# Making two of seven half-size products ahead for every pair of feature tiles, in place of the plain up-projection of a gated MLP, in an fp32 decoder trunk

## The chip, the cores and the metric

The kernel runs on one core of one Trainium2 chip. The metric is the device time of one launch in microseconds (us): the median of several runs of the same build. A profile is one execution recorded by the hardware profiler. Of the engines, PE is TensorE (matmuls; PEld is its weight load), DVE is VectorE, ACT is ScalarE, SP is SyncE, whose queue issues nearly all DMAs of this kernel.

## The reference

Two layers over 1024 tokens of width 1024, all in fp32. Layer 0 mixes tokens by gated recurrence and attention, layer 1 by pooling; each layer then has a gated MLP, and its up- and down-projection are what the change is about:

```python
h = x * (1.0 + sc2) + sh2                # x: after the mixer and a layer norm
u, v = jnp.split(h @ w_up, 2, axis=-1)   # w_up: 1024 x 5632, u and v: 1024 tokens x 2816
uc = conv_b                              # causal depthwise conv of width 3 along the tokens
for j in range(CONV_WIDTH):
    uc = uc + up[:, j:j + T] * conv_w[j]     # up: u with two zero rows ahead
y = (jax.nn.silu(uc) * v) @ w_down       # w_down: 2816 x 1024
x = _layer_norm(ALPHA * x + g2 * y, ln_g[l, 1], ln_b[l, 1])
```

The vectors `sc2`, `sh2`, `g2` and their like (adaLN) come from the conditioning vector `c` by a matrix of 1024 x 6144 per layer.

## The kernel before

Features lie on the 128 partitions and tokens along the row. The 1024 tokens are two halves of 512 (`hf` 0 and 1), the width 1024 is 8 tiles of 128 (`KT`), the 2816 features are 22 tiles (`FT`); tile `i` of u and of v make one gated feature tile. Every fp32 operand is split in a high part, a cast made by ACT (L261), and a low part, a subtraction made by DVE (L262). A product of two operands is three matmul passes (high by high, high by low, low by high), so a projection of 512 tokens to 128 features is 8 x 3 = 24 matmuls of 128x128 by 128x512.

**The plain up-projection.** `up` (L912) makes one feature tile for one half of the tokens: 24 matmuls into `pu`, the conv (`conv`, L896: ACT scales, DVE adds the two shifted terms, ACT applies silu), 24 matmuls into `pv`, a product with v on DVE, and a store of the result in DRAM (`hidden`). `STD = (5, 9)` of the 22 tiles go this way in layer 0 and in layer 1: 4 x 24 = 96 matmuls for one tile.

**The pairs.** The other 17 and 13 tiles go through `paired` (L971). It takes u and v of a tile and both halves of the tokens as a 2 by 2 block product, and makes it with seven half-size products instead of eight (Strassen's scheme, Winograd's form). Each is a `product` (L958) of 12 matmuls, and a tile is 84. The left factors are a11, a12, a22 (blocks of w_up) and s1 to s4 (sums of them, made by `pair_weights`, L218, on DVE); the right ones are b11, b21, b22 (blocks of h) and t1 to t4 (`forms`, L928: loaded again from DRAM, added on DVE, split). a11 b11 + a12 b21 is u of the first half. The results are put together by DVE: u2 and v2 are u and v of the second half, v1 is v of the first.

**Down.** `down` (L1012) loads `hidden` again (`load_hidden`, tiles `gh`, `gl`, `gt`), splits it, and multiplies with granules of w_down that are loaded and split once for each half of the tokens.

**Order.** The program is one long Python trace; the framework's scheduler keeps its own order on each engine. `weight` and `fetch` (L239, L253) load and split weights in the order of use, two ahead. Beside the main loop (L1173 to L1192) run generators: `tick` (L97) advances them at a rate given to `start`, and so lays their instructions between the matmuls. `norm_prep` and `between` (L1148, L1129) hold layer norm, pooling and `ffn_prep` (L871), which makes h of one half, splits it and stores it; for the second half they run beside the plain up-projection of the first, and `forms` beside that of the second. `fill` (L165) lays the making of adaLN vectors between the matmuls: one `ada_tile` is a DMA of 512 KB and a DVE reduce (L142), 96 in all. Tiles of 512 columns come from a pool `t2` of 25 buffers, staged weights from `ws` of 4, split weights from `wh` of 4, PSUM from two pools of 4 banks.

Of the kernel before, what the change touches and what calls it, by code (L numbers as in the profile page):

```python
# [17 lines left out]
P = 128  # L18
# [24 lines left out]
T2_BUFS = 25  # L43
# [9 lines left out]
STD = (5, 9)  # L53
FILL = 0.5
# [4 lines left out]
def trunk(ctx: ExitStack, tc: tile.TileContext, a: dict, out: bass.AP):  # L59
# [12 lines left out]
    def t2(name, w=HT):  # L72
        return tp.tile([P, HT + 16], F32, tag="t2", name=name, bufs=T2_BUFS)[:, :w]

# [22 lines left out]
    def tick():  # L97
        for item in list(active):
            item[2] += item[1]
            while item[2] >= 1:  # L100
                item[2] -= 1
                if next(item[0], active) is active:
                    active.remove(item)
                    break
# [75 lines left out]

    def parts(st, n=1024, hl=None):
# [4 lines left out]
        split(hl[0][:, :n], hl[1][:, :n], st[:, :n])  # L186
        return hl

# [10 lines left out]
    for l in range(DEPTH):  # L199
        for hf in range(NH):  # L200
            for i in range(STD[l]):
                worder += [("w_up", l, i), ("w_up", l, FT + i)]
        worder += [("pair", l, i) for i in range(STD[l], FT)]
# [7 lines left out]
    fetched = []  # L211

# [5 lines left out]
    def pair_weights(l, i):  # L218
# [3 lines left out]
        ga = parts(wa)  # L222
# [126 lines left out]
    def modulate(n, j, sv, tv, hl, act=False, keep=None):  # L349
# [7 lines left out]
        if keep is not None:  # L357
            nc.sync.dma_start(keep, hf)
# [495 lines left out]
    def outproj(hf):  # L854
        o = o_hl[hf]
        need((0, 2))
        rs_[hf] = r = [t2(f"r{hf}_{j}") for j in range(KT)]
# [13 lines left out]
    def ffn_prep(l, hf):  # L871
# [5 lines left out]
        h = hs[hf] = hl8(f"hf{l}{hf}")  # L877
        for j in range(KT):
            hsp[l, hf, j] = dram(f"h{l}{hf}{j}")
            rsp[l, hf, j] = dram(f"r{l}{hf}{j}")  # L880
            modulate(n[j], j, sv, tv, h, keep=hsp[l, hf, j])
            S.activation(n[j], n[j], AF.Identity, bias=col(bv, j), scale=col(av, j))
            nc.sync.dma_start(rsp[l, hf, j], n[j])
            yield
# [11 lines left out]
    def conv(l, i, u, first, last):  # L896

        uc = t2("uc")
# [13 lines left out]
    def up(l, hf, i):  # L912

        h = hs[hf]
        act = lambda k, hi: h[k][:, hi, :]
        pu = mm("pu")
        gemm(pu, weight("w_up", l, i), act, KT)
        tick()
        uc = conv(l, i, pu, uh[:, i, :] if hf else None, None if hf else uh[:, i, :])
        pv = mm("pv")  # L920
        gemm(pv, weight("w_up", l, FT + i), act, KT)
        V.tensor_tensor(uc, uc, pv, ALU.mult)
        nc.sync.dma_start(hidden(l, hf, i), uc)
        tick()

    right = {}

    def forms(l):  # L928

        for nm in ("t1", "t2", "t4", "t3"):  # L930
            right[nm] = []
        for k in range(HK):
            b11, b21, b12, b22 = (t2("hb") for _ in range(4))
            for t, (hf, kk_) in ((b11, (0, k)), (b12, (1, k)), (b22, (1, HK + k)), (b21, (0, HK + k))):
                nc.sync.dma_start(t, hsp[l, hf, kk_])
# [34 lines left out]

    def paired(l):  # L971
# [3 lines left out]
        low = [[(hs[hf][k][:, 0, :], hs[hf][k][:, 1, :]) for k in range(KT)] for hf in range(NH)]  # L975
        b11, b21, b22 = low[0][:HK], low[0][HK:], low[1][HK:]
        prev = None

        def ends(q):
            i, w, s1, y, z, u1, u2, v2, uc1 = q  # L980
            product(y, w["a22"], right["t4"], False, True)
            v1 = t2("v1")
            V.tensor_tensor(v1, s1, y, ALU.add)
            V.tensor_tensor(uc1, uc1, v1, ALU.mult)
            nc.sync.dma_start(hidden(l, 0, i), uc1)
            product(z, w["s4"], b22, False, True)
            V.tensor_tensor(u2, u2, z, ALU.add)
            uc2 = conv(l, i, u2, u1[:, HT - 2 : HT], None)
            V.tensor_tensor(uc2, uc2, v2, ALU.mult)
            nc.sync.dma_start(hidden(l, 1, i), uc2)  # L990

        for i in range(STD[l], FT):
            w = weight("pair", l, i, ahead=1)
            x, y, z = mm("px"), mm("py"), ax("pz")
            s1, u1, u2, v2 = (t2(nm) for nm in ("s1", "u1", "u2", "v2"))
            product(x, w["a11"], b11, True, True)
            S.copy(s1, x)
            product(y, w["s2"], right["t2"], True, True)
            V.tensor_tensor(u2, s1, y, ALU.add)
# [3 lines left out]
            product(x, w["a12"], b21, False, True)  # L1003
            S.copy(u1, x)
# [3 lines left out]
            uc1 = conv(l, i, u1, None, None)  # L1008
            prev = i, w, s1, y, z, u1, u2, v2, uc1
        ends(prev)  # L1010

    def down(l, hf):  # L1012
# [3 lines left out]
        g = []  # L1016

        def load_hidden():
# [7 lines left out]
        n = rs_[hf] = [t2(f"r{l}{hf}_{j}") for j in range(KT)]  # L1026
        for j0 in range(0, KT, 2):
# [237 lines left out]
```

## Time and profile before

| | |
|---|---|
| median of 3 runs | 1966.31 us (1966.2 to 1967.88) |
| the profiled execution, its own time | 1964.34 us |
| its span | 1962.5 us |
| mean granted clock of TensorE | 0.989 |
| PE busy | 1902.8 us (97%), 9558 matmuls |
| DVE busy | 1469.6 us (75%) |
| ACT busy | 821.5 us (42%) |
| DMA | 286.72 MB, 146 GB/s on average |

An engine's busy time is the time in which it carried out at least one instruction; instructions of one engine overlap a little, so the sum of their durations is larger. The chain of work that ended last goes back from the last instruction to what released each step, and gives each engine its share of the span. The 1.8 us between span and own time lie around the program.

### The profile page before, as it was taken

Reading aid. Unit: us, or ns where it says so; the run is one execution under the profiler, and the core shown is the slowest. Engines: PE = TensorE matmul, PEld = TensorE weight load, DVE = VectorE, ACT = ScalarE, POOL = GpSimd, SP = SyncE. Lnnn points to the kernel's source line nnn. Section 1 sums busy time; section 2 is a strip of 40 time slices with the busy share of each in tenths; the row PEclk is TensorE's granted clock in tenths of the full one; section 3 lists DMA queues with packets and bytes.
Section 4 is the critical chain, followed back from the end, with each engine's and each line's share of the span. In section 5 each row is a group of like instructions: output and inputs, shape, how many; then the busy total and the mean of one; then the engine's idle time right before and its main releaser. Section 6 shows DMA issues by size and latency. Waiting matters only on the chain.

```text
span 1962.5 us, 25481 instructions
## 1 busy us (share of the span) xinstructions
PE 1902.8 (97%) x9558; PEld 1590.4 (81%) x9558; DVE 1469.6 (75%) x2737; ACT 821.5 (42%) x1240; POOL 0.2 (0%) x4
## 2 busy tenths in 40 slices
PE   6999999999999999999999899998999999999996
PEld 6988988888788888888787678877888888888786
DVE  6897678778888787887755898998667777732846
ACT  4654254434664333343412435545434343422522
POOL 0000000000000000000000000000000000000000
PEclk9999999999999999999999899998999999999998
DMA  9522232234564333334775555336422222643731
GB/s 311 196 102 76 98 108 86 82 124 161 204 247 139 115 122 122 119 119 134 263 256 187 190 173 205 112 109 228 161 76 91 81 81 80 223 153 101 254 112 44
DMA packets 101932, 286.72 MB, mean 146 GB/s; under 512 B 12976, under 2 KB 15408, under 8 KB 101808
## 3 DMA queue, kind: packets, MB, share of 16 engines
q1 hardware_dynamic: 101232, 284.56, 42.4%
q8 instruction: 75, 1.23, 0.2%
q10 hardware_dynamic: 576, 0.52, 0.1%
q14 instruction: 49, 0.40, 0.1%
HBM read 241.00 MB, written 44.04 MB: 145 GB/s over the span
## 4 chain that ended last, share of the span: by engine, by line
PE 87%; DVE 6%; DMA 4%; ACT 2%; issue 1%; SPq 0%; DVEq 0%; ACTq 0%
PE pd L1039 20%; PE py L961 12%; PE pz L961 8%; PE px L961 8%; PE pu L271 8%; PE pv L271 7%; PE op L271 4%; PE zt L497 4%; PE att L740 3%; PE zt L395 2%; PE pd L271 2%; DMA wst<-g 2%; PE aq L271 1%; DVE whl L262 1%; PE pp L1123 1%
## 5 line engine op out<-in xcount | busy, mean ns | idle before, releaser
L261 ACT CAST whl<-wst 128x1024 fp32r<-128x1024 f32 (+1 forms) x267 | 271.5, 1029 | 477.8 <-PE pd L1039 180.1
L262 DVE TENSOR_TENSOR whl<-wst,whl 128x1024 fp32r<-128x1024 f32 (+1 forms) x267 | 316.0, 1194 | 92.9 <-ACT whl L261 91.6
L1039 PE MATMUL pd<-gh,whl 128*128 128x512 f32 x1024 | 322.1, 393 | 1.6 <-ACT gh L261 1.0
L961 PE MATMUL py<-t,whl 128*128 128x512 f32 x1080 | 258.1, 392 | 0.0
L961 PEld LDWEIGHTS py<-t,whl 128*128 128x128 f32 x1080 | 202.6, 188 | 45.2 <-DVE v L1006 0.6
L1039 PEld LDWEIGHTS pd<-gh,whl 128*128 128x128 f32 x1024 | 193.3, 189 | 43.9 <-ACT gh L261 1.7
L1039 PE MATMUL pd<-gl,whl 128*128 128x512 f32 x512 | 201.5, 393 | 8.4 <-DVE gl L262 8.4
L271 PE MATMUL pu<-hf,whl 128*128 128x512 f32 x672 | 166.0, 400 | 9.2 <-ACT uh L908 6.2
L961 PE MATMUL px<-hf,whl 128*128 128x512 f32 x720 | 173.8, 390 | 0.0
L271 PEld LDWEIGHTS pu<-hf,whl 128*128 128x128 f32 x672 | 129.5, 193 | 37.6 <-ACT uh L908 6.6
L961 PEld LDWEIGHTS px<-hf,whl 128*128 128x128 f32 x720 | 135.2, 188 | 29.1
L271 PE MATMUL pv<-hf,whl 128*128 128x512 f32 x672 | 158.5, 390 | 0.0
L142 DVE CUSTOM_DVE_ANT_0 adast<-adast,c 128x1024 f32<-128x1024 f32 x96 | 117.2, 1223 | 54.6 <-DMA adast<-in_ada_wT 54.4
L271 PEld LDWEIGHTS pv<-hf,whl 128*128 128x128 f32 x672 | 126.0, 188 | 26.3
L1039 PEld LDWEIGHTS pd<-gl,whl 128*128 128x128 f32 x512 | 96.9, 189 | 30.3 <-DVE gl L262 10.0
L1039 PE MATMUL pd<-gt,whl 128*128 128x512 f32 x432 | 102.6, 392 | 1.0 <-ACT gt L261 1.0
L497 PE MATMUL zt<-whl,h 128*128 128x256 f32 x768 | 100.7, 286 | 0.0
L902 DVE SCALAR_TENSOR_TENSOR uc<-u,cw,uc 128x511 f32<-128x511 f32 x120 | 89.8, 748 | 12.4 <-ACT uc L899 11.6
L1039 PEld LDWEIGHTS pd<-gt,whl 128*128 128x128 f32 x432 | 81.0, 188 | 19.2 <-ACT gt L261 1.4
L497 PEld LDWEIGHTS zt<-whl,h 128*128 128x128 f32 x768 | 94.4, 191 | 0.7 <-issue 0.3
L271 PE MATMUL op<-o,whl 128*128 128x512 f32 x384 | 91.8, 394 | 0.0
L961 PE MATMUL pz<-hf,gs 128*128 128x512 f32 x360 | 88.9, 395 | 0.0
(243 smaller groups left out, 2758.1 us busy)
## 6 DMA issues: line engine op xcount, KB each, us to landing
wst<-in_w_up SPq DMA_DIRECT2D x116, 512.0 KB, 3.5
adast<-in_ada_wT SPq DMA_DIRECT2D x96, 512.0 KB, 4.1
wst<-in_w_dn SPq DMA_DIRECT2D x64, 512.0 KB, 4.4
g<-uc SPq DMA_DIRECT2D x88, 256.0 KB, 2.0
wst<-g SPq DMA_DIRECT2D x44, 512.0 KB, 4.3
r<-r SPq DMA_DIRECT2D x64, 256.0 KB, 3.9
wst<-in_w_tok SPq DMA_DIRECT2D x28, 512.0 KB, 4.2
wst<-in_w_dn SPq DMA_DIRECT2D x32, 384.0 KB, 3.7
```

What stands on the lines that cost most here:

```text
L142: V.tensor_tensor_reduce(out=w, in0=w, in1=cb, scale=1.0, scalar=0.0, op0=ALU.mult, op1=ALU.add, accum_out=col(mods[l, ch], k),)
L261: S.copy(hi, src)
L262: V.tensor_tensor(lo, src, hi.bitcast(F32), ALU.subtract)
L271: PE.matmul(ps, w[wi][:, k * P : (k + 1) * P], act(k, hi), start=i == 0, stop=i == n - 1)
L395: PE.matmul(ps[t // 2][:, (t % 2) * 256 : (t % 2 + 1) * 256], h[k][:, hi, t * P : (t + 1) * P], w[wi][:, (k % 4) * 256 : (k % 4 + 1) * 256 ...
L497: PE.matmul(ps[:, u * 256 : (u + 1) * 256], h[k_][:, hi, (t + u) * P : (t + u + 1) * P], w[k_ // 4][wi][:, (k_ % 4) * 256 : (k_ % 4 + 1) * ...
L740: PE.matmul(ps[:, s], lhs[:, s], rhs[:, s], start=True, stop=True)
L902: V.scalar_tensor_tensor(uc[:, sh:], u[:, : HT - sh], cw, uc[:, sh:], ALU.mult, ALU.add)
L961: PE.matmul(ps, w[wi][:, k * P : (k + 1) * P], blk[k][hi], start=start and k == pi == 0, stop=stop and k == HK - 1 and pi == 2, skip_group ...
L1039: PE.matmul(ps[jj], w[jj][wi][:, (k - c0) * P : (k - c0 + 1) * P], act(k, hi), start=k == pi == 0, stop=k == sum(last_k) - 1 and pi == 2,)
L1123: PE.matmul(ps, wg[wi][:, b : b + P], o[k][:, hi, :], start=i == 0, stop=i == 5)
```

## The change

`STD` and `up` are gone: all 22 tiles of a layer go through the seven products. `EARLY = (16, 22)` tiles of each layer are cut in two. `early(l)` makes for each of them the two products a11 b11 and a12 b21, 24 matmuls, which need the first half of the tokens alone. It copies the first product (`s1`, ACT) and, after the second, u of the first half (`u1`, or for tiles from `EARLY_CONV = (0, 12)` on its conv result `uc`) and stores both in DRAM, by ACT's DMA queue. `paired(l)` loads them again and makes the other five products of these tiles, 60 matmuls ("late"), and all seven of the rest, six in layer 0.

In `paired`, ACT now copies s1 into the PSUM bank `y` ahead of s2 t2, and the matmuls add to it; DVE's additions of s1 (L983, L999, L1006) fall away, and ACT copies u2 and v2 out of PSUM. v2 + y, made by DVE, now has to be read before a22 t4 is added to the same bank.

Beside `early(l)` now run `norm_prep(1)` or `between(1)` and `forms` after it (`rest`), at the rates 1.5 and 2.5, and `issue_after` lays their instructions behind the split of the next weight. Smaller parts: `ffn_prep` of the second half doesn't split the four blocks that no product uses, and makes every other h of the first half on ACT; `pool_mix` makes `he` on ACT; `down` stores the low halves of w_down's granules in DRAM at the first half and loads them at the second (`again`), where before DVE made them a second time; `load_hidden` of the second half runs in the last quarter of the first; adaLN is filled at a rate of 0.65 (before 0.5) up to the MLP and 0.4 (before 0.2) in `paired`; `t2` has 19 buffers, a new pool `e2` 6.

```diff
+PIN = 1
+EARLY = (16, 22)
+EARLY_CONV = (0, 12)
-STD = (5, 9)
...
+    def again(src, key, n, hl):
...
+        nc.sync.dma_start(hl[1][:, :n].bitcast(F32), wlo[key])
+        st = wp.tile([P, 1024], F32, tag="ws", name="wst", bufs=WS_BUFS)
+        nc.sync.dma_start(st[:, :n], src)
+        S.copy(hl[0][:, :n], st[:, :n])
         return hl
...
+    def early(l):
+        b11, b21 = half_blocks(0)
+        prev = None
+        def end(q):
+            i, w, x = q
+            product(x, w[1], b21, False, True)
+            if i < EARLY_CONV[l]:
+                uc = e2("u1")
+                S.copy(uc, x)
+                S.copy(uh[:, i, :], uc[:, HT - 2 : HT])
+            else:
+                uc = conv(l, i, x, None, uh[:, i, :], e2("uc"))
+            kept[l, i, 1] = dram(f"e{l}{i}")
+            nc.scalar.dma_start(kept[l, i, 1], uc)
+        for i in range(EARLY[l]):
+            g = weight("w_up", l, i, ahead=min(3, EARLY[l] - i))
+            w = [tuple(z[:, q * 512 : (q + 1) * 512] for z in g) for q in range(2)]
+            behind[:] = splits.get(("w_up", l, i + PIN), [])
+            x, s1 = mm("px"), e2("s1")
+            product(x, w[0], b11, True, True)
+            S.copy(s1, x)
+            kept[l, i, 0] = dram(f"s{l}{i}")
+            nc.scalar.dma_start(kept[l, i, 0], s1)
+            if prev is not None:
+                end(prev)
+            prev = i, w, x
...
-        def ends(q):
-            i, w, s1, y, z, u1, u2, v2, uc1 = q
+        def end1(q):
+            i, w, y, z, u1, uc1, u2, v2 = q
             product(y, w["a22"], right["t4"], False, True)
-            v1 = t2("v1")
-            V.tensor_tensor(v1, s1, y, ALU.add)
-            V.tensor_tensor(uc1, uc1, v1, ALU.mult)
+            V.tensor_tensor(uc1, uc1, y, ALU.mult)
             nc.sync.dma_start(hidden(l, 0, i), uc1)
+        def end2(q):
+            i, w, y, z, u1, uc1, u2, v2 = q
             product(z, w["s4"], b22, False, True)
             V.tensor_tensor(u2, u2, z, ALU.add)
...
+        for i in range(FT):
+            late = i < EARLY[l]
+            w = weight("late" if late else "pair", l, i, ahead=1)
+            x, y, z = None if late else mm("px"), mm("py"), ax("pz")
+            u2, v2 = t2("u2"), t2("v2")
+            if late:
+                s1, u1 = nxt
+                nxt = load_kept(i + 1)
+                S.copy(y, s1)
+            else:
+                u1 = t2("u1")
+                product(x, w["a11"], b11, True, True)
+                S.copy(y, x)
+                if prev is not None:
+                    end1(prev)
+            product(y, w["s2"], right["t2"], False, True)
+            S.copy(u2, y)
             if prev is not None:
-                ends(prev)
+                (end1 if late else end2)(prev)
             product(z, w["s1"], right["t1"], True, True)
+            S.copy(v2, z)
+            if late:
+                if prev is not None:
+                    end2(prev)
+            else:
+                product(x, w["a12"], b21, False, True)
+                S.copy(u1, x)
             product(y, w["s3"], right["t3"], False, True)
-            V.tensor_tensor(v2, s1, y, ALU.add)
-            V.tensor_tensor(v2, v2, z, ALU.add)
+            V.tensor_tensor(v2, v2, y, ALU.add)
...
+                    if hf == 0 and j0 == KT - 2 and k % 2:
+                        load_hidden(nxt, 1)
...
     for l in range(DEPTH):
-        for hf in range(NH):
-            if hf:
-                finish(pb_)
-                pb_ = start(forms(l), 0.7)
-            for i in range(STD[l]):
-                up(l, hf, i)
+        early(l)
         finish(pb_)
-        pace[0] = 0.2
+        pace[0] = 0.4
         paired(l)
```

The order of instructions moves at two places. The first is DVE in the middle of `paired(0)`: what it does between one addition of a product in `pz` and the next addition of one in `py`. `whl` and `gs` are low halves of weights, `wsum` the sums of weight blocks, `cw0` the conv weights. Before:

```order
L987 TENSOR_TENSOR u2_6366<-u2_6366,pz_6363 128x512
L150 TENSOR_TENSOR mod05_92<-mod05_92,ada_bT_81 128x8
L902 SCALAR_TENSOR_TENSOR uc_6568<-u2_6366,cw0_641,uc_6568 128x511
L904 SCALAR_TENSOR_TENSOR uc_6568<-u1_6365,cw0_641,uc_6568 128x1
L902 SCALAR_TENSOR_TENSOR uc_6568<-u2_6366,cw0_641,uc_6568 128x510
L262 TENSOR_TENSOR whl_6494<-wsum_6488,whl_6494 128x1024
L904 SCALAR_TENSOR_TENSOR uc_6568<-u1_6365,cw0_641,uc_6568 128x2
L224 TENSOR_TENSOR wsum_6632<-wst_6627 128x512
L225 TENSOR_TENSOR wsum_6632<-wsum_6632,wst_6625 128x512
L262 TENSOR_TENSOR whl_6497<-wst_6483,whl_6497 128x1024
L989 TENSOR_TENSOR uc_6568<-uc_6568,v2_6367 128x512
L1006 TENSOR_TENSOR v2_6509<-s1_6506,py_6504 128x512
```

The same piece after the change, in a late tile:

```order
L1076 TENSOR_TENSOR u2_6624<-u2_6624,pz_6623 128x512
L297 TENSOR_TENSOR gs_6730<-s4_6721,gs_6730 128x512
L251 TENSOR_TENSOR wsum_6828<-wst_6826 128x512
L946 SCALAR_TENSOR_TENSOR uc_6798<-u2_6624,cw0_641,uc_6798 128x511
L948 SCALAR_TENSOR_TENSOR uc_6798<-uh_701,cw0_641,uc_6798 128x1
L946 SCALAR_TENSOR_TENSOR uc_6798<-u2_6624,cw0_641,uc_6798 128x510
L948 SCALAR_TENSOR_TENSOR uc_6798<-uh_701,cw0_641,uc_6798 128x2
L1109 TENSOR_TENSOR v2_6736<-v2_6736,py_6733 128x512
L252 TENSOR_TENSOR wsum_6828<-wsum_6828,wst_6824 128x512
L1078 TENSOR_TENSOR uc_6798<-uc_6798,v2_6625 128x512
```

Six instructions now stand between the addition to u2 and the one to v2, where ten stood; the conv of u2 is still ahead of the latter.

The second is ACT at the passage from `down(0, 0)` to `down(0, 1)`. Granules of 768 columns are the last of a pair of output tiles, `gh` is hidden of the second half. Before:

```order
L261 CAST whl_9197<-wst_9195 128x768
L261 CAST whl_9202<-wst_9200 128x768
L261 CAST whl_9261<-wst_9259 128x1024
L261 CAST whl_9266<-wst_9264 128x1024
L261 CAST gh_9334<-wst_9332 128x1024
L261 CAST gh_9340<-wst_9338 128x1024
L261 CAST whl_9324<-wst_9322 128x1024
L261 CAST whl_9329<-wst_9327 128x1024
L261 CAST gh_9346<-wst_9344 128x1024
```

And after the change:

```order
L297 CAST gh_9344<-wst_9342 128x1024
L297 CAST gh_9362<-wst_9360 128x1024
L297 CAST gh_9380<-wst_9378 128x1024
L297 CAST gh_9398<-wst_9396 128x1024
L297 CAST whl_9404<-wst_9402 128x768
L297 CAST whl_9411<-wst_9409 128x768
L297 CAST gh_9430<-wst_9428 128x1024
L297 CAST gh_9448<-wst_9446 128x1024
L297 CAST gh_9466<-wst_9464 128x1024
L297 CAST gh_9484<-wst_9482 128x1024
L199 CAST whl_9488<-wst_9490 128x1024
```

Eight casts of hidden now stand ahead of the second half's first granule (`whl_9488`, made by `again`), which itself came ahead of all of them before.

## Rows read from the trace of the kernel before

**Rows 1.** The page: busy times and shares of the chain that ended last.

```profile
PE 1902.8 (97%) x9558; PEld 1590.4 (81%) x9558; DVE 1469.6 (75%) x2737; ACT 821.5 (42%) x1240; POOL 0.2 (0%) x4
PE 87%; DVE 6%; DMA 4%; ACT 2%; issue 1%; SPq 0%; DVEq 0%; ACTq 0%
```

**Rows 2.** Chain of waits, plain up-projection of both layers: start, us, what.

```profile
507.13 7.33 PE pu L271 x24
...
581.57 5.44 PE pv L271 x24
...
1220.99 5.49 PE pu L271 x24
...
1345.41 8.29 PE pu L271 x24
```

**Rows 3.** Chain of waits, one pair of layer 0, and the end of layer 1's.

```profile
641.64 5.60 PE pz L961 x24
647.24 2.76 PE px L961 x12
...
660.99 5.60 PE pz L961 x24
...
1697.82 110.42 PE pd L1039 x485
```

**Rows 4.** Timeline of PE, end of layer 0's pairs: start, us, engine, line, operation, tiles.

```profile
949.38 0.40 PE L1039 MATMUL pd<-gl,whl 128*128 128x512 f32 x1
```

**Rows 5.** Windows: stretch, length, busy (instructions) of PE, PEld, DVE, ACT, POOL; clock; DMA share, GB/s.

```profile
619.60:953.00 333.40, 333.40 (x1449) 271.68 (x1448) 269.30 (x409) 134.15 (x175) 0.00 (x0) 1.00 0.37 125
1221.00:1345.00 124.00, 115.39 (x508) 93.53 (x507) 117.02 (x202) 64.21 (x93) 0.00 (x0) 0.98 0.38 133
```

**Rows 6.** Timeline of DVE: layer norm, pooling and plain up-projection of layer 1.

```profile
1249.46 4.87 DVE L333 TENSOR_TENSOR r<-r,rstd 128x512 f32<-128x512 f32 x8 [0.86 <-PE rstd L330]
1254.25 0.54 DVE L1093 TENSOR_SCALAR he<-r,v,v 128x512 f32<-128x512 f32 x1
1254.70 1.23 DVE L262 TENSOR_TENSOR whl<-wst,whl 128x1024 fp32r<-128x1024 f32 x1
1255.84 0.69 DVE L1103 TENSOR_TENSOR he<-he 128x512 f32<-128x512 f32 x1
...
1260.51 0.75 DVE L902 SCALAR_TENSOR_TENSOR uc<-pu,cw,uc 128x511 f32<-128x511 f32 x1
1261.17 0.18 DVE L1092 COPY he<-hh 128x16 f32<-128x16 f32 x1
```

**Rows 7.** Groups of instructions: out<-in, count, busy, mean ns, idle before and releaser.

```profile
L261 ACT CAST whl<-wst 128x1024 fp32r<-128x1024 f32 (+1 forms) x267 | 271.5, 1029 | 477.8 <-PE pd L1039 180.1
L142 DVE CUSTOM_DVE_ANT_0 adast<-adast,c 128x1024 f32<-128x1024 f32 x96 | 117.2, 1223 | 54.6 <-DMA adast<-in_ada_wT 54.4
L997 ACT COPY s<-px 128x512 f32<-128x512 f32 x30 | 17.6, 587 | 83.1 <-PE px L961 83.0
L860 ACT ACTIVATE r<-r 128x512 f32<-128x512 f32 x16 | 9.6, 627 | 5.9 <-DMA r<-in_xT 5.9
```

**Rows 8.** Timeline of ACT's queue near the end: four DMA issues.

```profile
1957.84 1.86 ACTq L1145 DMA_DIRECT2D out_x<-r  x4
```

**Rows 9.** Timeline of one pair: product s3 t3, conv's first step, addition to v2.

```profile
707.88 2.88 PE L961 MATMUL py<-t,whl 128*128 128x512 f32 x12
...
709.65 0.82 ACT L899 ACTIVATE uc<-u,cb,cw 128x512 f32<-128x512 f32 x1
...
711.22 0.68 DVE L1006 TENSOR_TENSOR v<-s,py 128x512 f32<-128x512 f32 x1
```

**Rows 10.** What PE waited for: us in total, times, longest.

```profile
PE pd L1039 <- DVE gl L262: 8.4, 4, 5.2
PE varp L322 <- DVE lnss L317: 8.4, 2, 5.6
```

**Rows 11.** Chain of waits, down-projection of layer 0.

```profile
978.78 83.61 PE pd L1039 x366
...
1101.28 7.96 PE pd L1039 x26
```

**Rows 12.** Windows of PE alone: stretch, length, busy, clock, DMA share, GB/s.

```profile
1080.00:1100.00 20.00, 13.74 (x54) 0.87 0.60 198
1820.00:1840.00 20.00, 18.77 (x81) 1.00 0.63 212
1840.00:1860.00 20.00, 20.00 (x95) 1.00 0.93 340
```

More of the change, by code (lines that the diff above doesn't have):

```diff
@@ L101, in tick @@
                 item[2] -= 1
-                if next(item[0], active) is active:
+                with ExitStack() as order:
+                    for i in behind:
+                        order.enter_context(tc.issue_after(i.ins))
+                    over = next(item[0], active) is active
+                if over:
                     active.remove(item)
@@ L185, in parts @@
             hl = (t[:, 0, :], t[:, 1, :])
-        split(hl[0][:, :n], hl[1][:, :n], st[:, :n])
+        made[:] = split(hl[0][:, :n], hl[1][:, :n], st[:, :n])
         return hl
+    made = []
+    behind = []
     worder = []
@@ L199, in trunk @@
     for l in range(DEPTH):
-        for hf in range(NH):
-            for i in range(STD[l]):
-                worder += [("w_up", l, i), ("w_up", l, FT + i)]
-        worder += [("pair", l, i) for i in range(STD[l], FT)]
+        worder += [("w_up", l, i) for i in range(EARLY[l])]
+        worder += [("late", l, i) for i in range(EARLY[l])]
+        worder += [("pair", l, i) for i in range(EARLY[l], FT)]
         for hf in range(NH):
@@ L211, in trunk @@
     fetched = []
+    splits = {}
     def stage(src):
@@ L876, in ffn_prep @@
         sv, tv, av, bv = vecs[l, 4]
-        h = hs[hf] = hl8(f"hf{l}{hf}")
+        h = hs[hf] = [None if hf and j < HK else two(a4(f"hf{l}{hf}_{j}")) for j in range(KT)]
         for j in range(KT):
@@ L894, in hidden, with conv @@
         return hid[l, hf, i // 2][:, (i % 2) * HT : (i % 2 + 1) * HT]
-    def conv(l, i, u, first, last):
-        uc = t2("uc")
+    def conv(l, i, u, first, last, uc=None):
+        if uc is None:
+            uc = t2("uc")
         S.activation(uc, u, AF.Identity, bias=col(cvb[l], i), scale=col(cvw[l], 2 * FT + i))
@@ L910, in conv @@
         return uc
[L912 to L924, printed above, removed]
     right = {}
@@ L969, in product, with half_blocks @@
         tick()
+    def half_blocks(hf):
+        b = [h if h is None else (h[:, 0, :], h[:, 1, :]) for h in hs[hf]]
+        return b[:HK], b[HK:]
+    kept = {}
+    def early(l):
[24 more added lines that the diff above has]
+            prev = i, w, x
+        behind.clear()
+        end(prev)
@@ L971, in paired, with load_kept @@
     def paired(l):
-        low = [[(hs[hf][k][:, 0, :], hs[hf][k][:, 1, :]) for k in range(KT)] for hf in range(NH)]
-        b11, b21, b22 = low[0][:HK], low[0][HK:], low[1][HK:]
+        b11, b21 = half_blocks(0)
+        _, b22 = half_blocks(1)
         prev = None
-        def ends(q):
-            i, w, s1, y, z, u1, u2, v2, uc1 = q
+        def load_kept(i):
+            if i < EARLY[l]:
+                t = e2("s1"), e2("u1")
+                for q in range(2):
+                    nc.sync.dma_start(t[q], kept[l, i, q])
+                return t
@@ L987, in ends @@
             V.tensor_tensor(u2, u2, z, ALU.add)
-            uc2 = conv(l, i, u2, u1[:, HT - 2 : HT], None)
+            uc2 = conv(l, i, u2, uh[:, i, :] if i < EARLY[l] else u1[:, HT - 2 : HT], None)
             V.tensor_tensor(uc2, uc2, v2, ALU.mult)
             nc.sync.dma_start(hidden(l, 1, i), uc2)
[L992 to L999, printed above, removed]
+        for i in range(FT):
[7 more added lines that the diff above has]
+                S.copy(y, s1)
+            else:
+                u1 = t2("u1")
[5 more added lines that the diff above has]
+            S.copy(u2, y)
@@ L1190, in trunk @@
         if l < DEPTH - 1:
-            pb_ = start(between(1), 2.5)
+            pb_ = start(rest(between(1), 1), 2.5)
     finish()
```

94 lines of the change are left out of this document (63 added, 31 removed).

## The prediction

> **What bounds the kernel now.** I read the page first. PE is busy for 97% of the span and holds 87% of the chain that ended last [rows 1]; DVE is at 75%, ACT at 42%. Whatever takes matmuls away shortens the kernel, so long as DVE, next in line, keeps up with the shorter stages. So I read each stage's speed from the chain of waits, then DVE's share of it in windows, and last what PE waited for.
>
> In the plain up-projection 24 matmuls take 5.44 us, 0.2267 each [rows 2]. A tile for both halves is four such runs, 21.76 us. Among the pairs, two runs into `pz` begin at 641.64 and 660.99 [rows 3]: 19.35 us for 84 matmuls, 0.2304 each. In that stretch PE never stops and DVE is busy for 269.3 of 333.4 us, 81% [rows 5]. So a pair costs 2.41 us less than a plain tile, not the 2.72 that twelve matmuls would give at 0.2267. Elsewhere PE is less sheltered: beside `between(1)` it was busy for 115.4 of 124.0 us and DVE for 117.0, 94% [rows 5], and its largest waits for DVE are 8.4 us for `gl` in down and 8.4 us in a layer norm [rows 10].
>
> **The change part by part.** I counted instructions per stage in the order of the built program, and priced them by the distance from one start to the next [rows 6]: 0.60 for 512 columns of DVE (eight in 4.79 us), 1.14 for a low half of 1024, 0.45 for a scale and shift, 0.66 for a conv term. A reduce for adaLN lasts 1.22 [rows 7], 1.15 with the same overlap.
>
> *Matmuls.* The up-projection loses 168 (3864 to 3696): 14 tiles leave the plain form, 14 x 2.41 = 33.7 us. [...]
>
> *Layer 0's up-projection.* Before, it ran from 507.13 [rows 2] to 949.38 [rows 4]: 442.3 us. Now it has three pieces.
> - `early(0)`: 16 x 24 = 384 matmuls x 0.2304 = 88.5; with 7 short ones of layer norm at 0.23, 90.2 us of PE. DVE has 71 x 0.60 + 25 x 0.66 + 14 x 1.14 + 8 x 0.45 and small ones for 2.4, 81 us, at the 94% that it reached beside `between` 86. ACT has 46 activations x 0.63, 16 casts x 1.03, 33 copies or half casts x 0.59 [rows 7], 65 us, and issues 28 DMAs; four issues took 1.86 us [rows 8], so 13 more: 78, or 83 at 94%. PE is the longest, narrowly; I take 92 for handing over.
> - 16 late tiles of 60 matmuls: 60 x 0.2304 = 13.82, together 221.1. Six full pairs: 116.1.
> - From `early` into `paired` PE needs t2 and the first late weights; by the counts both are made some 5 to 9 us of DVE time ahead. I take 2, bounds 0 and 9.
> Sum 431.2, so **-11.1**.
>
> *Layer 1's.* Before, from 1220.99 [rows 2] to 1697.82 [rows 3]: 476.8. Now `early(1)` has 528 matmuls, 121.6, and 62 of pooling and layer norm, 14.3 at 0.23: 136 us of PE. DVE has 125 x 0.60 + 29 x 0.66 + 24 x 1.14 + 8 x 0.45 + 5.4 = 131, at 94% 139. ACT comes to 117 with its 41 issues, 124 at 94%. DVE bounds by a little: 139. With 22 x 13.82 = 304.0 and 2 for handing over, 445, so **-31.8**. The bounds of this stage are PE alone (136) and DVE's durations added without overlap (156).
>
> *Inside a late tile.* DVE has 9 x 0.60 + 2 x 0.66 + 2 x 1.14, two reduces and small ones: 11.6 of 13.82 us, 84%, where a pair of before had 81% and no wait. Three additions with s1 are gone; ACT's copies in their place cost 0.59 [rows 7] (writing PSUM is in no row; the bounds are the 0.59 of a copy out of PSUM and the 0.82 of the scaling for the conv [rows 9]), and ACT has 6 us of work in 13.8. The copy of s1 into `y` stands about a tile ahead in ACT's order, and three other banks of PSUM cover it; if not, up to 1.2 us per tile would show.
>
> The new wait is v2 + y. PE may not begin a22 t4 into that bank before DVE has read it. In the order before, two products (5.5 us) stood between s3 t3 and that point; now one does, s2 t2 of the next tile, 2.76 us [rows 3]. Before, the addition began 0.6 us after the product: 707.88 with 2.72 to its successor is 710.60, and DVE begins at 711.22 [rows 9]. Now, as the first order excerpt shows, the conv of u2 stands ahead of it. s4 b22 ends 2.72 before s3 t3 ends; then come u2 + z (0.6, and 0.2 to start), ACT's scaling (0.82), 1.6 of conv, 0.6 of v2 + y, and 0.6 in hand-overs: it ends some 1.5 us after s3 t3, 1.2 before PE wants it. A weight's low half or a reduce ahead of it (1.14, 1.15) uses that up alone. Queued behind the matmul are all later products, so a wait is lost in full. I take 0.1 us for each of 38 late tiles: **+4**, bounds 0 and the slow rival below.
>
> *Down.* Between 1080 and 1100 PE was busy for 13.74 of 20 us at a granted clock of 0.87 [rows 12], and then 26 matmuls took 7.96 us [rows 11], where at 83.61 / 366 = 0.2284 they take 5.94. So 8.3 us are to be had at the passage from `down(0, 0)` to `down(0, 1)`: 6.3 idle, 2.0 of clock. The change loads and splits `gh` there in advance (the second order excerpt), takes the 24 low halves (27 us) and, by the order, 48 reduces (55 us) from DVE. What is late next is the DMA. In the last quarter of `down(0, 0)` 132 matmuls (30.1 us) run beside 11 loads of hidden (0.524 MB each), 2.88 MB of w_down and 2.88 MB of low halves stored: 11.5 MB. The best 20 us of the trace moved 340 GB/s [rows 12], at which this takes 33.9 us: 3.8 late at worst, of which I take 1, since the first buffers are what PE wants first. [...] **-7** in layer 0. In layer 1 PE idles for 1.2 of 20 us at this passage [rows 12], and the same 1 us may be late: **0**.
>
> *Mixer.* adaLN at 0.65 lays 13 more reduces beside the first 500 us, 15 us of DVE spread over a stretch where it isn't the bound; six loads of x come earlier, and `t2` has six buffers fewer. **+2**, bounds 0 and 6.
>
> The sum is -11.1 - 31.8 + 4 - 7 + 0 + 2 = -43.9: 1964.3 - 43.9 = 1920.4 of the profiled execution's own time. The median of the runs lies 2.0 above that execution; I forecast **1922** for the median.
>
> **The rivals.**
> - *The early stages are bound by DVE or ACT.* For it: DVE at 94% beside `between`, and PE idle for 7% there [rows 5]; after such a wait 24 matmuls took 8.29 us [rows 2] where 5.44 is usual. Against it: the second half's four unused blocks aren't split any more, and `he` went to ACT. With durations that don't overlap, `early(1)` takes 156, 17 more, and `early(0)` some 100, 8 more: 1947. Chance 0.18.
> - *Down is bound by DMA.* Low halves add 2.88 MB in each quarter of `down` at the first half as stores, and as loads at the second. If each of the four stages loses the 3.8 us of above: 1922 + 15 = 1937. For it: down had the profile's highest traffic already. Against it: 340 GB/s was moved with PE busy throughout [rows 12]. Chance 0.1.
> - *The wait for v2 + y comes in place of the gain (slower).* One mechanism at one place: a22 t4 in 38 late tiles. The gain is used up when each loses 44 / 38 = 1.2 us, which is when v2 + y ends over 4.0 us after s3 t3 instead of 1.5: a low half and a reduce both ahead of it do it. At 2 us each: 1922 + 38 x 2 - 4 = 1994. For it: DVE at 84%. Against it: PE waits for nothing among the pairs of before [rows 5], and the scheduler put only short rows between. Chance 0.08, and 0.04 more that it stops short of that and the time stays the same.
>
> **How the numbers follow.** The forecast itself has 0.6, and its bounds (handing over, 0 to 9 twice; mixer 0 to 6; early(1) at 136; late tiles at 0) put it between 1908 and 1935. A measurement can tell about 0.2%, 4 us, from no change. All cases but the slow one and that of equal time are faster: 0.88; same 0.04; slower 0.08. The range runs from 1904 (everything at its better bound, with 4 us of other waits of rows 10 gone) to 1950, which takes in both milder rivals and leaves out the late tiles' stalls.
>
> **What would show it.** Right: 60 matmuls per late tile in 13.8 us with no wait of PE for `v` or `py`; `early(0)` near 92 us and `early(1)` near 139 with DVE above 90%; no gap at the passage in `down(0)`. Wrong: a wait of PE for DVE `v` in the list of waits, over 40 us in all; a granted clock below 0.95 in the early stages; `gl` or a DMA before PE in down.

## The result, and the profile after

The changed kernel takes 1938.87 us (median of 4 runs, 1934.68 to 1940.62), the kernel before 1966.26 beside it: a ratio of 0.9858, interval 0.9839 to 0.9877. That is 27.4 us faster. The forecast was 1922 in a range of 1904 to 1950; the direction and the range held, the gain is 62% of the forecast's. The profiled execution is the fastest of the four (1934.68).

The page of the changed kernel, busy times and the shares of the chain, to be read beside [rows 1]:

```profile
span 1932.9 us, 25673 instructions
...
PE 1866.4 (97%) x9390; PEld 1553.2 (80%) x9390; DVE 1389.3 (72%) x2651; ACT 897.4 (46%) x1408; POOL 0.2 (0%) x4
...
PE 83%; DVE 8%; DMA 4%; ACT 2%; issue 2%; SPq 0%; DVEq 0%; ACTq 0%
```

PE has 168 matmuls less and is 36.4 us less busy, yet the span fell by 29.6: PE stands idle for 66.5 us of it, 59.7 before. DVE's share of the chain grew from 6% to 8%. To see where PE waits, the span is cut by the first matmul of each stage. The timeline of PE in the changed kernel gives the starts of `early(0)`, `paired(0)`, `down(0, 0)`, `early(1)`, `paired(1)` and `down(1, 0)`:

```profile
512.72 0.73 PE L999 MATMUL px<-hf,whl 128*128 128x512 f32 x2 [3.47 <-ACT whl L297]
...
608.46 2.96 PE L999 MATMUL pz<-t,whl 128*128 128x512 f32 x12
...
953.04 0.39 PE L1145 MATMUL pd<-gh,whl 128*128 128x512 f32 x1
...
1210.44 5.63 PE L999 MATMUL px<-hf,whl 128*128 128x512 f32 x24
...
1363.51 5.76 PE L999 MATMUL pz<-t,whl 128*128 128x512 f32 x24
...
1668.36 0.39 PE L1145 MATMUL pd<-gh,whl 128*128 128x512 f32 x1
```

Against the starts of before, 507.13, 949.38, 1220.99 and 1697.82 [rows 2 to 4], and with each late tile's term put to its layer:

| stage | before | after | change | predicted |
|---|---|---|---|---|
| mixer, up to the MLP | 507.1 | 512.7 | +5.6 | +2 |
| layer 0, up-projection | 442.3 | 440.3 | -1.9 | -9.4 |
| layer 0, down | 271.6 | 257.4 | -14.2 | -7 |
| layer 1, up-projection | 476.8 | 457.9 | -18.9 | -29.5 |
| layer 1, down | 264.7 | 264.5 | -0.1 | 0 |
| span | 1962.5 | 1932.9 | -29.6 | -43.9 |

The late tiles are as forecast. Three rows of the chain of waits hold one of them (three products into `py`, two into `pz`):

```profile
648.37 8.29 PE py L999 x36
656.66 5.56 PE pz L999 x24
662.22 8.29 PE py L999 x36
```

13.85 us for 60 matmuls, 13.82 forecast. The early stages aren't: 95.7 and 153.1 us where 92 and 139 stood. This is what PE waited for between 1205 and 1390, and in the second fence between 500 and 640:

```profile
PE px L999 <- ACT uh L952: 12.6, 3, 7.8
```

```profile
PE px L999 <- ACT whl L297: 3.5, 1, 3.5
PE px L999 <- ACT s L1039: 2.1, 1, 2.1
PE py L999 <- ACT whl L297: 1.9, 1, 1.9
PE py L999 <- DVE v L1109: 1.6, 1, 1.6
PE px L999 <- ACT uh L952: 1.4, 1, 1.4
PE py L999 <- DVE whl L297: 1.2, 1, 1.2
```

`uh` (L952) is ACT's copy of the last two columns of u, the last reader of a bank `px` after the conv. ACT is named, but what ACT waits for is DVE: the copy comes after the conv's two terms (L946), and these stand behind other work in DVE's order. Windows of the changed kernel (columns as in [rows 5]), DVE's timeline of the same stretch, and what ended the longest of the three waits:

```profile
1310.00:1320.00 10.00, 5.94 (x17) 4.43 (x16) 8.17 (x13) 8.60 (x15) 0.00 (x0) 0.66 1.01 378
1320.00:1330.00 10.00, 10.00 (x45) 8.24 (x45) 5.97 (x9) 5.02 (x9) 0.00 (x0) 1.00 1.01 343
1330.00:1340.00 10.00, 9.27 (x41) 7.33 (x41) 10.00 (x17) 8.82 (x16) 0.00 (x0) 1.00 1.04 403
1340.00:1350.00 10.00, 3.28 (x15) 2.35 (x13) 10.00 (x16) 4.59 (x8) 0.00 (x0) 0.87 0.11 40
1350.00:1360.00 10.00, 8.96 (x33) 7.32 (x34) 10.00 (x16) 6.15 (x12) 0.00 (x0) 0.79 0.62 232
```

```profile
1312.78 1.53 DVE L946 SCALAR_TENSOR_TENSOR uc<-px,cw,uc 128x511 f32<-128x511 f32 x2
...
1325.39 0.69 DVE L975 TENSOR_TENSOR hb<-hb 128x512 f32<-128x512 f32 x1 [4.00 <-DMA hb<-h]
...
1348.26 0.74 DVE L946 SCALAR_TENSOR_TENSOR uc<-px,cw,uc 128x511 f32<-128x511 f32 x1
...
1350.05 1.40 DVE L946 SCALAR_TENSOR_TENSOR uc<-px,cw,uc 128x510 f32<-128x510 f32 x2
```

```profile
1350.83 0.16 ACT L952 COPY uh<-px 128x2 f32<-128x2 f32 x1 [3.64 <-DVE uc L946]
...
1351.04 12.63 PE L999 MATMUL px<-hf,whl 128*128 128x512 f32 x48 [7.76 <-ACT uh L952]
```

The first wait, 4.1 us up to 1315, comes before any form: the conv terms it needs stand behind the layer norm and the making of h, and run at 1312.78. The longest, 7.8 us, comes from what follows. DVE stands idle for 4 us because h, just stored, is still being loaded for the forms, with all DMA engines busy (a share of 1.01 in 1320 to 1330); then the forms come in one stretch, and the last conv terms on which a bank depends, at 1348.26 and 1350.05, come after them. PE stands still from 1343 to 1351. And behind each of the two long stops the granted clock was low: in 1310 to 1320 it was 0.66, and 17 matmuls took 5.94 us; in 1350 to 1360 it was 0.79, and 33 took 8.96.

### The profile page after: what moved, and what is told of

It is laid out like the page before. It is cut to its first block, busy times and chain, and to the rows that moved or that the text cites. A ratio compares the mean times of both kernels' runs of the same rounds, so it can differ in the third digit from the quotient of the medians.

```text
span 1932.9 us, 25673 instructions
## 1 busy us (share of the span) xinstructions
PE 1866.4 (97%) x9390; PEld 1553.2 (80%) x9390; DVE 1389.3 (72%) x2651; ACT 897.4 (46%) x1408; POOL 0.2 (0%) x4
## 4 chain that ended last, share of the span: by engine, by line
PE 83%; DVE 8%; DMA 4%; ACT 2%; issue 2%; SPq 0%; DVEq 0%; ACTq 0%
PE pd L1145 23%; PE py L999 18%; PE pz L999 12%; PE px L999 9%; PE zt L532 4%; PE op L306 3%; PE att L775 3%; DMA adast<-in_ada_wT 2%; PE zt L430 2%; PE pd L306 2%; DVE whl L297 1%; PE aq L306 1%; PE pp L1231 1%; DVE adast L152 1%; PE af L306 1%
## 5 line engine op out<-in xcount | busy, mean ns | idle before, releaser
L999 PE MATMUL py<-t,whl 128*128 128x512 f32 x1584 | 374.5, 392 | 5.6 <-ACT whl L297 1.9
L999 PEld LDWEIGHTS py<-t,whl 128*128 128x128 f32 x1584 | 296.4, 188 | 75.6 <-DVE v L1109 3.3
L297 ACT CAST whl<-wst 128x1024 fp32r<-128x1024 f32 (+1 forms) x196 | 200.3, 1033 | 283.8 <-PE pd L1145 114.2
L297 DVE TENSOR_TENSOR whl<-wst,whl 128x1024 fp32r<-128x1024 f32 (+1 forms) x196 | 233.1, 1199 | 104.8 <-ACT whl L297 104.1
L999 PE MATMUL px<-hf,whl 128*128 128x512 f32 x1056 | 254.0, 397 | 20.1 <-ACT uh L952 14.0
L999 PEld LDWEIGHTS px<-hf,whl 128*128 128x128 f32 x1056 | 201.0, 191 | 65.4 <-ACT uh L952 15.7
L999 PE MATMUL pz<-t,whl 128*128 128x512 f32 x528 | 130.3, 395 | 0.0
L999 PE MATMUL pz<-hf,gs 128*128 128x512 f32 x528 | 129.1, 393 | 0.0
L999 PEld LDWEIGHTS pz<-t,whl 128*128 128x128 f32 x528 | 99.2, 188 | 23.6
L999 PEld LDWEIGHTS pz<-hf,gs 128*128 128x128 f32 x528 | 99.1, 188 | 22.7
L953 ACT ACTIVATE uc<-uc 128x512 f32<-128x512 f32 x88 | 55.8, 634 | 91.9 <-DVE uc L948 76.1
L946 DVE SCALAR_TENSOR_TENSOR uc<-u,cw,uc 128x511 f32<-128x511 f32 x124 | 92.4, 745 | 5.4 <-ACT uc L943 5.2
```

Of the source, the lines that this page charges most:

```text
L297: return S.copy(hi, src), V.tensor_tensor(lo, src, hi.bitcast(F32), ALU.subtract)
L946: V.scalar_tensor_tensor(uc[:, sh:], u[:, : HT - sh], cw, uc[:, sh:], ALU.mult, ALU.add)
L953: S.activation(uc, uc, AF.Silu)
L999: PE.matmul(ps, w[wi][:, k * P : (k + 1) * P], blk[k][hi], start=start and k == pi == 0, stop=stop and k == HK - 1 and pi == 2, skip_group ...
```

## The experiments

Differences to the changed kernel are between medians; the kernel before, run beside each group, had 1966.26 (with the changed kernel), 1966.74 (e1 to e4), 1966.26 (e5 to e8) and 1964.49 (e9 to e12). Builds whose program is the same up to the MLP start it between 510.1 (e3) and 516.6 us (e5) in their profiles, so a stage is compared by its length.

### What makes the early stage of layer 1 long: e1, e2, e9

**e1.** The conv of tiles 12 to 21 leaves the early stage.

```diff
-EARLY_CONV = (0, 12)
+EARLY_CONV = (0, 22)
```

> The changed kernel with the conv of layer 1's tiles 12 to 21 moved out of the early stage into the late tiles (EARLY_CONV 0, 22). Theory A (the early stage of layer 1 is bound by the amount of work on DVE and ACT; its 12.6 us of waits for ACT uh are px banks held by a conv that queues behind that work): ten convs are 13 us of DVE and some 9 of ACT, the waits for uh go to under 4 us and the kernel is 8 to 13 us faster than the changed one; the late tiles of layer 1 stay at 13.85 us. Theory B (a serial tail: layer norm, h stored, h loaded, forms; the early products only wait because they are few): the wait moves to the first late tile (py or pz waiting for t), and the time moves by less than 4 us.

1930.24 us, ratio 0.9819 (0.9803 to 0.9835): 8.6 us under the changed kernel. The early stage of layer 1 lasts 139.8 us (1211.03 to 1350.78). The whole stage in the changed kernel and, in the second row, in e1:

```profile
1210.44:1363.51 153.07, 140.32 (x606) 113.14 (x604) 139.03 (x230) 101.08 (x167) 0.00 (x0) 0.96 0.58 206
1211.03:1350.78 139.75, 136.66 (x606) 110.46 (x604) 120.92 (x203) 92.48 (x156) 0.00 (x0) 1.00 0.63 218
```

That the 139 of the forecast comes out here is chance: it stood for DVE as the bound, with the conv, and in e1 PE's own 136.7 us and 2.9 of waits fill the stage, with DVE at 87%. What PE still waited for there and at the start of the late tiles:

```profile
PE py L999 <- ACT py L1089: 4.8, 1, 4.8
PE px L999 <- ACT s L1039: 1.8, 1, 1.8
PE px L999 <- ACT u L1026: 1.1, 1, 1.1
```

The 12.6 us for `uh` are gone; 4.8 came back at the first late tile, as a wait for s1 (theory B had one there for t). The conv's place in the early stage cost what theory A says. That it is DVE's total, as A put it, isn't shown: DVE had idle time in that stretch, and e1 takes away both the work and the banks that wait for it.

**e2.** The generator beside the stage runs faster, 3.5 for 2.5.

```diff
-            pb_ = start(rest(between(1), 1), 2.5)
+            pb_ = start(rest(between(1), 1), 3.5)
```

> The changed kernel with the generator beside the early stage of layer 1 at a rate of 3.5 instead of 2.5, no work more or less. Theory A (amount of work): within 2 us of the changed kernel, the waits only move. Theory B (serial tail that starts late): forms start some 10 us earlier, and 5 to 10 us are gained.

1943.06 us (0.9882, 0.9867 to 0.9897), 4.2 slower than the changed kernel. The stage lasts 152.9 us, the loads for the forms begin 106.0 us into it (108.2 in the changed kernel), and PE waits 11.9 us for `uh` and `s` there. Theory B falls in this form: a higher rate doesn't start the tail 10 us sooner; in the changed kernel DVE was busy for 92% of the stage ahead of it (99.45 of 108.20 us). The loss lies outside the stage: in the profile, the pairs of layer 1 take 309.4 us for 304.9, and the MLP begins 3.5 later.

**e9.** To part the bank from the work: ACT copies u out of the bank, DVE's work stays.

```diff
+                u = x
+                if l:
+                    u = t2("u1")
+                    S.copy(u, x)
-                uc = conv(l, i, x, None, uh[:, i, :], e2("uc"))
+                uc = conv(l, i, u, None, uh[:, i, :], e2("uc"))
```

> The changed kernel, in whose early stage of layer 1 ACT copies u of tiles 12 to 21 out of PSUM at once and the conv reads the copy: DVE's work stays, ACT has ten copies more (6 us), only the PSUM bank px is freed without waiting for DVE. Theory A (PE's 12.6 us of waits for ACT uh are banks held by convs that stand behind the forms in DVE's order): those waits fall under 4 us, the early stage of layer 1 shortens from 153 by some 8 us or more, though part may come back as a wait for the first late tile. Rival (the amount of DVE work bounds the stage): its length stays within 2 us of 153, the wait only gets another name.

1952.76 us (0.9937, 0.9923 to 0.9952), 13.9 slower, and the stage lasts 164.3 us (1212.84 to 1377.09). PE's waits in it:

```profile
PE px L999 <- ACT u L1032: 24.1, 2, 19.4
```

The copy itself came late. ACT's timeline of that stretch in e9:

```profile
1315.82 1.03 ACT L297 CAST whl<-wst 128x1024 fp32r<-128x1024 f32 x1
1325.74 1.34 ACT L297 CAST t<-hb 128x512 fp32r<-128x512 f32 x2 [8.89 <-DVE hb L975]
...
1329.61 0.58 ACT L1032 COPY u<-px 128x512 f32<-128x512 f32 x1
```

The bank's reader stands behind the casts of the forms in ACT's order, and these wait for the h that is being loaded: ACT was idle for 8.9 of the 19.4 us in which PE waited for it. Neither expectation held. But the wait is one of place in e9, not of the amount of work. That the same is true of the changed kernel, where DVE was busy in the last of the waits and idle ahead of it, is likely and not shown; an order with the bank's reader first wasn't tried.

### What shortened down: e3, e5, e6

**e3.** Low halves of w_down made twice by DVE, as before.

```diff
-                if hf == 0:
-                    w = wgran(src, n * P)
...
-                else:
-                    w = again(src, (l, j, c0), n * P, hl)
+                w = wgran(src, n * P, hl)
```

> The changed kernel with w_down's low halves made by DVE in both halves as before, not stored in DRAM and loaded again. Theory A (the 14 us that the down stages of layer 0 gained come from DVE's relief by again): 6 to 14 us slower, with waits of PE for gl or whl at the passage. Theory B (they come from the hidden tiles loaded ahead and from the adaLN reduces that left): within 2 us, or up to 4 us faster for the DMA that is gone (46 MB of low halves).

1939.89 us (0.9867, 0.9853 to 0.9882): 1.0 more, no difference. Down of layer 0 lasts 258.6 us against 257.4. Storing low halves gains nothing that a run here can show.

**e5.** No hidden tiles loaded ahead (the condition on L1152 is false).

```diff
-                    if hf == 0 and j0 == KT - 2 and k % 2:
+                    if False:
```

> The changed kernel without the loads of the second half's hidden tiles in the last quarter of down's first half; they are loaded when the second half begins, as before. Theory A (these loads close the passage from down(0, 0) to down(0, 1), which is most of the 14 us that layer 0's down gained): 5 to 10 us slower, with waits of PE for gl or whl at the passage. Theory B (the adaLN reduces that left down do it): within 2 us.

1949.26 us (0.9919, 0.9904 to 0.9934), 10.4 more. Down of layer 0 is 263.1, that is 5.7 longer, and down of layer 1 268.6, 4.1 longer: theory A. (In its profile the MLP also began 3.9 later, ahead of the edit.) As down of layer 1 is as long after the change as before, something else in it must cost there what these loads gain; which part is open.

**e6.** The rates of adaLN as before, so that reduces run in down again.

```diff
-FILL = 0.65
+FILL = 0.5
...
-        pace[0] = 0.4
+        pace[0] = 0.2
```

> The changed kernel with adaLN filled at the rates of before (0.5 up to the MLP, 0.2 among the pairs), so that some 48 reduces run in down(0, 0) and down(0, 1) again. Theory A (hidden loaded ahead does it): within 3 us. Theory B (the reduces that left DVE do it): down of layer 0 is 5 to 10 us longer, with the layer norm beside down(0, 1) late. In both the late tiles of layer 0, with half the reduces, stay at 13.85 us.

1947.58 us (0.9905, 0.9891 to 0.992), 8.7 more, although the MLP begins 4.2 us earlier (508.57): down of layer 0 takes 269.2, 11.8 longer. So both theories hold a part, and the larger one is the reduces, of which 29 ran there, not 48. But DVE, which theory B names, isn't full. The windows of down(0, 0) in e6 and, in the second fence, of the changed kernel:

```profile
953.00:1080.00 127.00, 121.81 (x527) 98.03 (x525) 78.52 (x103) 37.74 (x40) 0.00 (x0) 1.00 0.91 321
```

```profile
953.00:1080.00 127.00, 127.00 (x556) 103.88 (x556) 59.95 (x63) 44.57 (x47) 0.00 (x0) 1.00 0.76 272
1080.00:1100.00 20.00, 19.95 (x95) 16.31 (x94) 16.05 (x37) 10.88 (x16) 0.00 (x0) 1.00 0.63 216
```

DVE is at 62% in e6, the DMA engines at 91%. In this window PE waits 2.9 us for parts of `hidden` (`gh`, `gt` and low halves), and from 1080 on 4.8 us for `whl` and the loaded low halves. A reduce brings 512 KB; that these loads, beside those of the low halves, make the others late is likely, but no run has the reduces without the low halves' traffic. In the changed kernel PE waits for nothing in down of layer 0, and the passage of [rows 12] (13.74 of 20 us, clock 0.87) is closed.

### The new wait in a late tile: e7, e8

**e7, e8.** v2 + y is followed by + y and - y, once and twice, so that the bank is read longer.

```diff
             V.tensor_tensor(v2, v2, y, ALU.add)
+            for op in (ALU.add, ALU.subtract) * (1 if late else 0):
+                V.tensor_tensor(v2, v2, y, op)
```

> The changed kernel with v2 + y followed by + y and - y in every late tile: two more DVE reads of the bank, 1.2 us, before a22 t4 may begin. Theory A (the wait for v2 + y is met with a slack of 1.15 us, read from the trace: v2 + y ends 1.6 us after s3 t3, a22 t4 begins 2.76 after): PE waits 0 to 0.4 us per late tile, the kernel is 0 to 12 us slower than the changed one. Rival (DVE at 86% has no reserve, any added work is lost in full): 38 x 1.2 = 45 us slower.

1947.88 us (0.9898, 0.9873 to 0.9923; 1939.98 to 1949.47): 9 more, inside theory A's 0 to 12, with 4.3 us of waits of PE for `v`. But it is no test of theory A's slack, for PE's order isn't that of the changed kernel any more:

```profile
653.59 5.69 PE L999 MATMUL py<-t,whl 128*128 128x512 f32 x24
659.12 2.03 PE L999 MATMUL pz<-t,whl 128*128 128x512 f32 x8
661.23 3.04 PE L999 MATMUL py<-t,whl 128*128 128x512 f32 x12
664.10 1.11 PE L999 MATMUL pz<-t,whl 128*128 128x512 f32 x4
```

The 24 are s3 t3 and s2 t2 of the next tile, the 12 into `py` a22 t4: eight matmuls of s1 t1 now stand ahead of it, so that 20 cover the reads, not 12. And only part of the 9 us lies among the late tiles: in the profile the pairs are 2.4 and 3.7 us longer, down of layer 1 2.9 and the mixer 2.3.

> The same with four more reads, 2.4 us. Theory A: PE waits 2.4 - 1.15 = 1.25 us in each late tile, 38 x 1.25 = 47 us over the changed kernel, so some 20 us slower than the kernel before: the point from which the slow rival of the prediction decides lies between this and two reads. Rival: 90 us over the changed kernel.

1943.56 us (0.9892, 0.9875 to 0.9908): 5 more, where 47 were expected. Theory A is wrong for this run, and why stands in PE's order: the scheduler lays the program out anew for each build. In the order of the built program, in the changed kernel, a22 t4 of a tile follows s3 t3 after one product, s2 t2 of the next tile. With four more reads it comes two or three products later, within s3 t3 of the next tile (a mark ' is the next tile's):

```
changed kernel:  py s3 t3, py' s2 t2, py a22 t4, pz' s1 t1, pz s4 b22
e8:              py s3 t3, py' s2 t2, pz' s1 t1, pz s4 b22, py' s3 t3 (part), py a22 t4
```

The cover grew from 2.76 to over 8 us, and DVE, busy for 173.1 of 175 us in 640 to 815, still kept pace. So the wait isn't priced by a fixed distance; both builds with more reads got more cover. What happens once DVE has no time left, no run shows.

### What else: e4, e10, e11, e12

**e4.** One yield for three per tile where h of the first half is made.

```diff
             yield
-            yield
-            yield
+            if hf:
+                yield
+                yield
```

> The changed kernel with one yield instead of three per tile in the making of h of the first half (both layers), so that its work and stores are laid as closely as before. Theory A (the early stage of layer 0 starts 5.6 us later than the up-projection before because the last loads of x wait for buffers that this slower making of h frees late, and ACT's first weight cast stands behind them): it starts 3 to 5 us earlier, 3 to 5 us faster in all. Theory B (the smaller pool t2 or ACT's extra work does it): within 1 us.

1940.98 us (0.9877, 0.9861 to 0.9894): 2 more. The early stage starts at 510.23, inside the spread of the others: a miss, theory A isn't borne out.

**e10.** e1, with the first late tile's s1 and u1 loaded while the last early tile is made (`load_kept` moved out of `paired`).

```diff
+            if i == EARLY[l] - 1:
+                first[:] = load_kept(l, 0)
...
-        nxt = load_kept(0)
+        nxt = tuple(first)
```

> e1_conv_late with s1 and u1 of the first late tile loaded while the last early tile is made, instead of behind the late weights' loads. Theory (the 4.8 us that PE waited for ACT's copy of s1 into py in e1 is this load's place in SP's queue): the wait in layer 1 goes, 3 to 5 us faster than e1_conv_late, some 1926; layer 0 gains under 1 us. Rival (the passage is bound by forms or late weights on DVE): within 1.5 us of e1_conv_late, the wait moves to DVE.

1926.23 us (0.9798, 0.9783 to 0.9812): 4.0 under e1, 12.6 under the changed kernel, the fastest version. PE's wait at that place, 4.8 us in e1, is 1.5: the load's place in SP's queue was most of the cause.

**e11.** e10 with adaLN at 0.5 up to the MLP and 0.5 among the pairs.

> e10 with adaLN at 0.5 up to the MLP, as before the change, and 0.5 among the pairs, so that all reduces are still done ahead of down. Theory (the mixer's 5 us come from 13 more reduces and their loads beside it): the early stage of layer 0 starts near 508.5 instead of 510 to 516, the late tiles of layer 0 (DVE 86% to some 90%) keep 13.85 us, and the kernel is 3 to 5 us faster than e10. Rival (the start depends on something else, or the late tiles can't take more reduces): within 2 us of e10 or slower.

1930.93 us (0.9822, 0.9805 to 0.9838), 4.7 over e10 where 3 to 5 less were expected. The early stage does start at 509.05, as e6's did at 508.57, the two earliest of all; some 3 to 4 us of the mixer are the filling rate's, as far as two executions can tell. But the pairs of layer 0, 345.2 us in e10, take 350.6, with 4.9 us of waits for `v`: those late tiles can't carry more reduces, as the rival has it.

**e12.** The kernel before, two plain tiles of layer 1 made pairs.

```diff
-STD = (5, 9)
+STD = (5, 7)
```

> The kernel before with two of layer 1's plain tiles as pairs (STD 5, 7): 24 matmuls fewer and nothing else. Theory (a removed matmul gives what a pair saves, 21.76 - 19.35 = 2.41 us per tile): 4.8 us faster than before. [...] Rival (with fewer plain tiles the forms of layer 1 come late): 0 or slower, with a wait of PE for t in the first pair.

1971.28 us against 1964.49 (1.0029, 1.0018 to 1.004): slower, as only the rival with late forms allows, but not by its cause. The forms weren't late; what PE waited for between 1215 and 1460 is the layer norms of `between(1)`:

```profile
PE varp L322 <- DVE lnss L317: 10.4, 1, 10.4
PE rstd L330 <- DVE lny L286: 2.9, 1, 2.9
PE pu L271 <- DVE hf L356: 2.8, 1, 2.8
```

19.6 us of waits there, 9.0 in the same window of the kernel before: 10.6 more, less the 4.8 of the matmuls, is 5.8 of the 6.8 us. Fewer plain tiles, it seems, leave too little for PE beside `between(1)`. The price of a matmul could not be read from this run, though its pairs ran at the pace of before (19.28 us from the `pz` run at 1608.93 to that at 1628.21, 19.27 in the kernel before).

## Why the prediction was right or wrong

**Right: what a matmul is worth.** 13.85 us per late tile of 60, 0.231 each, where the forecast had 0.2304. Right, too, that the late tiles bear the new wait. From the product's end at 706.38 (703.62 plus a third of 8.29) to the end of the addition in the same tile

```profile
703.62 8.45 PE L999 MATMUL py<-t,whl 128*128 128x512 f32 x36
...
707.31 0.68 DVE L1109 TENSOR_TENSOR v<-v,py 128x512 f32<-128x512 f32 x1
```

are 1.6 us, 1.5 forecast; in the 38 late tiles PE waited for `v` twice, 1.6 and 0.2 us, where the term had 4. The larger wait, in the first late tile of layer 0, had a cause that the prediction didn't name. DVE stood at `wsum`, ahead of v2 + y in its order, for a weight that took 6.34 us to land:

```profile
618.60 6.34 DMA wst<-in_w_up
```

```profile
625.03 0.69 DVE L251 TENSOR_TENSOR wsum<-wst 128x512 f32<-128x512 f32 x1 [3.87 <-DMA wst<-in_w_up]
625.64 0.68 DVE L1109 TENSOR_TENSOR v<-v,py 128x512 f32<-128x512 f32 x1
...
626.38 3.04 PE L999 MATMUL py<-t,whl 128*128 128x512 f32 x12 [1.55 <-DVE v L1109]
```

**Right by halves: the slow rival.** It priced the wait by one fixed product of cover; e7 and e8 show that the order isn't fixed.

**Wrong: `early(1)`, "DVE bounds by a little: 139".** It took 153.1, 14 more, which is the first rival's 156 nearly (chance 0.18). The step that failed is the stage as one sum of DVE's work over 94%. The sum was short: DVE was busy for 139.0 us, not 131, which over 94% would be 148. And its order counts. PE waited for banks whose conv terms stood first behind the layer norm and h, then behind the forms, which came in a lump after DVE had been idle while h went out and came back, with 343 to 403 GB/s moved. 12.6 us of waits and 3.6 of clock (17 matmuls in 5.94 us instead of 3.9, 33 in 8.96 instead of 7.5) make 16.2, which with 136 of PE's own work is 152.2. Which weighs more, the amount or the order, stays open: e1 takes away both, and e9 didn't part them. The trace of before had the sign:

```profile
PE pu L271 <- ACT uh L908: 6.2, 1, 6.2
```

It is the wait that ended at 1345.41, ahead of the slow 24 matmuls of [rows 2], in the same stage. As ACT is named, it isn't among the waits for DVE that the prediction lists [rows 10]; there, too, the conv terms stood behind the making of h in DVE's order.

**Wrong: handing over and `early(0)`.** "I take 2, bounds 0 and 9": 344.6 less 16 x 13.85 and 6 x 19.31 is 7.1 in layer 0; in layer 1, 304.9 less 22 x 13.85 is 0.2. `early(0)` took 95.7 for 92, of which 4.1 are waits. I counted t2 and late weights as made. The weights weren't: of the 7.1 us, PE waited 1.9 and 1.2 for `whl` of the second late tile, 1.6 for v and 0.6 for the copy of s1. The sums of that tile's weights came on DVE at 614.00, behind six conv terms of the last early tiles.

**Wrong by a term's size: down, -14.2 for -7.** I took the idle time of the passage only and then charged 1 us for DMA. e5 and e6 show two parts: loading hidden ahead (5.7 us) and the reduces' absence (11.8 us without it, not additive, as the whole is 14.2). The prediction had 48 reduces there, 55 us of DVE; the trace of before has some 30, and by e6 it is likely their loads that matter, not DVE. The charge of 1 us wasn't due: PE waited for nothing, and 340 GB/s isn't the ceiling that I made it: ten microseconds of the changed kernel moved 403.

**Wrong by a term's size: mixer, +5.6 for +2**, just inside its bounds of 0 and 6, which is chance: other builds start up to 3.9 us later. Part is the filling rate (e6, e11); the rest varies from one execution to the next by more than it weighs.

The errors went both ways: 3.6, 7.5 and 10.6 us too good, 7.2 too bad. Without the last the time would have been 1946, near the end of the range. And the bounds of the forecast, given as 1908 to 1935, add up to 1909 to 1940 (7 more for each handing over and 4 for the mixer above, 13 less below): the measured 1938.87 lies above the former and inside the latter.

## What to carry to other kernels

A stage whose engines are each below their capacity can still be late by its tail: look for a chain that goes through memory and back, and for what stands behind it in an engine's order while holding a buffer that the busiest engine wants. Work that waits for nothing (here the conv) is best taken out of such a stage into one that has room, and loads that begin the next stage belong ahead of its other loads. And the engine that a wait names need not be the one to relieve: look at what that engine itself waited for. Before pricing a wait by the distance between two instructions, ask whether the scheduler keeps that distance.

## What the runs showed of the hardware that I hadn't expected

The 16 DMA engines moved 403 GB/s in 1330 to 1340 us of the changed kernel, where the best stretch of the kernel before, cut in tens from 0 (1700 to 1710), moved 364. And the stop of 4.06 us ahead of 1315.24 cost more than 4.06 us: the granted clock was 0.66 in the ten microseconds with the stop, and the 17 matmuls in it took 0.349 us each, not the 0.227 of [rows 2]. From PE's restart at 1315.2 to 1319 the granted clock was 0.50; from 1321 it was 1.00 again.
